# FFN up and gate projections by seven block products in place of eight

## The chip, the cores and the metric

The kernel runs on one core of a Trainium2 chip. The metric is the time of one execution on the device in microseconds (us). A core has TensorE (PE, matrix products into PSUM banks), VectorE (DVE), ScalarE (ACT), GpSimd (POOL) and SyncE (SP), whose queue issues nearly all transfers between the device's memory and the core's SBUF. Each engine runs its own queue in order and waits on semaphores.

## The reference

One layer of a hybrid decoder for a prompt of 2048 tokens and 8 single-token samples, model width 1024, FFN width 2816, in float32. The part that the change touches:

```python
h = rmsnorm(x, g_ffn) * (1.0 + scale_f) + shift_f
u = h @ w_up_conv
gv = h @ w_up_gate
uc, s_conv_ffn_new = causal_dwconv(u, s_conv_ffn, conv_ffn_w, conv_ffn_b)
f = (jax.nn.gelu(uc) * gv) @ w_down
x = x + gate_f * f
```

Ahead of it stand an input projection (`w_in`), a retention block over chunks of 128 tokens, an RG-LRU block and an output projection (`w_out`).

## The kernel before

Tokens are in three groups of 704, 640 and 704 + 8 columns (groups 0, 1 and 2 below), each cut into two token blocks of 352, 320 and 356 columns. A group runs through the whole layer before the next one starts; features are on the partitions, tokens on the free axis.

A float32 product is made of three passes. Each operand is split into a high part, rounded to the format in which TensorE runs fast, and the low rest. `mm3` (L284) adds high x high, high x low and low x high into one bank. For an output tile of 128 rows and a token block, `proj` (L508) does so for eight k of 128 features: 24 matmuls.

Weights come in units of 512 KB, two ahead of their use. In group 0 `fetch` (L245) loads the unit, ScalarE makes the high part (L277), GpSimd the low one (L278), and SyncE stores both (1 MB) in device memory (L281); groups 1 and 2 load that 1 MB (L250). SyncE's store waits for GpSimd, with later loads behind it.

The FFN works on 22 tiles, two of which make a pair `i`. `up_item` (L799) takes a product out of its bank on ScalarE, does the convolution on VectorE (L809) and GeLU on ScalarE; `gate_item` (L821) multiplies it with the gate product and splits the result (L366 on ScalarE, L367 on GpSimd). `down_item` (L736) multiplies a pair's two tiles with `w_down` for one of 8 output tiles m and one block, 6 matmuls, and adds the result to x (L745 on VectorE). Down of pair i - 1 stands between the items of pair i.

At the FFN's start `norm2` (L774) sums the squares, forms the norm factor, spreads it with a small product (`bc2`), and `hnorm` (L468) makes the two parts of h. Block 1's operands are made while TensorE works on block 0 of the first two tiles (four items). The order of each engine's queue comes from a list of items in program order (`group_items`, L883), priorities and a scheduler's own model. The next group's x is brought in and transposed by `xload` (L416), listed at pair 4, into buffers of its own.

## Time and profile before

| | us |
|---|---|
| median of 3 runs | 2534.19 (2534.02 to 2536.27) |
| the profiled execution, whole | 2540.24 |
| its span, first to last instruction | 2538.3 |

The profile has the busy time of each engine, its share of the span, and groups of instructions by line: out <- in by the program's names, partitions x elements, count, then busy us and mean ns of one, then the engine's idle time just before them and what ended it. PEclk is the granted clock of TensorE as a share of the full one. Durations of matmuls overlap, so the pace of a stretch is its length over its count.

### The profile page before, as it was taken

The numbers are of one execution on the slowest core, as the hardware profiler recorded it, in microseconds if no ns is written. First come the engines' busy times: TensorE is split into PE (matmuls) and PEld (weight loads), VectorE is DVE, ScalarE is ACT, GpSimd is POOL, SyncE is SP. The second block draws the span as 40 slices with busy tenths as digits, with TensorE's granted clock in tenths as the row PEclk, the third lists the DMA queues.
The fourth block names the chain that finished last, engine by engine and source line by source line (L and its number), as shares of the span: only waits on it lengthen the run. The fifth ranks groups of instructions, "written<-read, shape, count | busy, mean of one in ns | idle before, by whom it ended". The sixth has DMA issues, their size and how long they took to land. (4 is left out here: it accounts for less than half of the span.)

```text
span 2538.3 us, 38920 instructions
## 1 busy us (share of the span) xinstructions
PE 2467.1 (97%) x15875; PEld 2388.5 (94%) x15875; DVE 1283.0 (51%) x3009; ACT 728.2 (29%) x1422; POOL 667.3 (26%) x641
## 2 busy tenths in 40 slices
PE   6999999999999999999999999999999899999997
PEld 4888888999999999999999999999998899999997
DVE  4744578433433465558433333456676734334335
ACT  4422345233233242224311111322222421111112
POOL 2444445343343342223100000222222300000010
PEclk8999999999999999999999999999999999999999
DMA  9575655666566553342444444353332243333432
GB/s 328 160 262 195 211 177 199 219 209 206 183 224 209 173 200 120 133 152 101 171 150 149 150 149 150 133 191 118 126 118 101 93 158 117 150 133 117 150 138 92
DMA packets 143223, 413.39 MB, mean 163 GB/s; under 512 B 8281, under 2 KB 88293, under 8 KB 105405
## 3 DMA queue, kind: packets, MB, share of 16 engines
q1 hardware_dynamic: 141943, 410.15, 46.5%
q8 instruction: 125, 2.05, 0.3%
q10 hardware_dynamic: 974, 0.49, 0.1%
q14 instruction: 53, 0.43, 0.1%
q0 software_dynamic: 128, 0.26, 0.0%
HBM read 297.18 MB, written 113.82 MB: 162 GB/s over the span
## 5 line engine op out<-in xcount | busy, mean ns | idle before, releaser
L285 PE MATMUL proj<-hh,w 128*128 128x352 f32 (+2 forms) x3264 | 1049.7, 323 | 14.0 <-DVE hh L504 7.3
L286 PE MATMUL proj<-hl,w 128*128 128x352 f32 (+2 forms) x3264 | 1051.0, 322 | 4.6 <-DVE hl L486 2.6
L287 PE MATMUL proj<-hh,w 128*128 128x352 f32 (+2 forms) x3264 | 1046.3, 321 | 0.0
L285 PEld LDWEIGHTS proj<-hh,w 128*128 128x128 f32 x3264 | 616.5, 189 | 25.9 <-ACT hh L491 7.9
L286 PEld LDWEIGHTS proj<-hl,w 128*128 128x128 f32 x3264 | 615.7, 189 | 10.8 <-DVE hl L486 4.9
L287 PEld LDWEIGHTS proj<-hh,w 128*128 128x128 f32 x3264 | 616.6, 189 | 1.0 <-issue 0.4
L745 DVE SCALAR_TENSOR_TENSOR x<-down,mod,x 128x352 f32<-128x352 f32 (+3 forms) x720 | 409.1, 570 | 206.0 <-PE down L287 204.8
L285 PE MATMUL down<-ffh,w 128*128 128x352 f32 (+2 forms) x1056 | 342.8, 325 | 8.2 <-DVE x L745 8.0
L367 POOL TENSOR_TENSOR ffl<-cv,ffh 128x352 fp32r<-128x352 f32 (+2 forms) x132 | 123.7, 937 | 822.8 <-ACT ffh L366 822.8
L287 PE MATMUL down<-ffh,w 128*128 128x352 f32 (+2 forms) x1056 | 338.5, 321 | 0.0
L286 PE MATMUL down<-ffl,w 128*128 128x352 f32 (+2 forms) x1056 | 338.4, 320 | 0.0
L278 POOL TENSOR_TENSOR w<-wr,w 128x1024 fp32r<-128x1024 f32 x96 | 232.0, 2423 | 364.6 <-ACT w L277 333.6
L807 DVE COPY oc<-u 128x2 f32<-128x2 f32 x132 | 37.0, 280 | 347.0 <-ACT u L804 347.0
L825 DVE TENSOR_TENSOR cv<-cv,proj 128x352 f32<-128x352 f32 (+2 forms) x132 | 67.4, 510 | 283.4 <-PE proj L287 281.4
L285 PEld LDWEIGHTS down<-ffh,w 128*128 128x128 f32 x1056 | 199.9, 189 | 10.8 <-DVE x L745 10.1
L804 ACT ACTIVATE u<-proj 128x352 f32<-128x352 f32 (+2 forms) x132 | 60.4, 458 | 512.9 <-PE proj L287 512.9
L286 PEld LDWEIGHTS down<-ffl,w 128*128 128x128 f32 x1056 | 200.2, 190 | 0.0
L287 PEld LDWEIGHTS down<-ffh,w 128*128 128x128 f32 x1056 | 200.0, 189 | 0.0
L277 ACT ACTIVATE w<-wr 128x1024 fp32r<-128x1024 f32 x98 | 102.6, 1056 | 262.7 <-issue 108.3
L809 DVE SCALAR_TENSOR_TENSOR cv<-u,vec,cv 128x352 f32<-128x352 f32 (+3 forms) x264 | 155.9, 591 | 33.7 <-ACT cv L805 27.2
L366 ACT ACTIVATE ffh<-cv 128x352 fp32r<-128x352 f32 (+2 forms) x132 | 64.3, 487 | 223.3 <-DVE cv L825 223.3
L818 ACT ACTIVATE cv<-cv 128x352 f32<-128x352 f32 (+2 forms) x132 | 64.6, 490 | 154.6 <-DVE cv L809 122.2
(220 smaller groups left out, 2630.3 us busy)
## 6 DMA issues: line engine op xcount, KB each, us to landing
w<-w_in SPq DMA_DIRECT2D x48, 1024.0 KB
w<-w_up_conv SPq DMA_DIRECT2D x44, 1024.0 KB
w<-w_up_gate SPq DMA_DIRECT2D x44, 1024.0 KB
w<-w_down SPq DMA_DIRECT2D x44, 1024.0 KB
w_in<-w SPq DMA_DIRECT2D x24, 1024.0 KB
w_up_conv<-w SPq DMA_DIRECT2D x22, 1024.0 KB
w_up_gate<-w SPq DMA_DIRECT2D x22, 1024.0 KB
w_down<-w SPq DMA_DIRECT2D x22, 1024.0 KB
```

The lines of the kernel that those rows point to most:

```text
L277: S.activation(out=wh, in_=r_, func=AF.Copy)
L278: lo_on.tensor_tensor(out=wl, in0=r_, in1=wh.bitcast(F32), op=ALU.subtract)
L285: T.matmul(out, wh, xh, start=first, stop=False)
L286: T.matmul(out, wh, xl, start=False, stop=False)
L287: T.matmul(out, wl, xh, start=False, stop=last)
L366: S.activation(out=hi[:, 0:n], in_=src, func=AF.Copy)
L367: G.tensor_tensor(out=lo[:, 0:n], in0=src, in1=hi[:, 0:n].bitcast(F32), op=ALU.subtract)
L745: V.scalar_tensor_tensor(out=xs, in0=q[:, 0:np_], scalar=modv[:, jg, m, 0:1], in1=xs, op0=ALU.mult, op1=ALU.add)
L804: S.activation(out=u[:, 2:2 + n], in_=q, func=AF.Copy)
L809: V.scalar_tensor_tensor(out=cv[:, 0:np_], in0=u[:, j:j + np_], scalar=cfw[:, j, ft:ft + 1], in1=cv[:, 0:np_], op0=ALU.mult, op1=ALU.add)
L818: S.activation(out=cv[:, 0:n], in_=cv[:, 0:n], func=AF.Gelu_apprx_tanh)
L825: V.tensor_tensor(out=cv, in0=cv, in1=q, op=ALU.mult)
```

## The change

Weights and h of a pair are taken as 2 x 2 blocks: A11, A12 (first tile; k 0 to 3 and 4 to 7), A21, A22 (second tile); b11, b21 (token block 0, the two halves of k), b12, b22 (block 1). Seven products of sums give all four outputs (tile, block): S1 = A21 + A22, S2 = S1 - A11, S3 = A11 - A21, S4 = A12 - S2 on the weights' side, t1 = b12 - b11, t2 = b22 - t1, t3 = t2 - b11, t4 = b21 - t2 on the other. Each is four k, 12 matmuls. P1, P6, P7 and P4 add up in bank x, P5 and P3 in bank z, P2 in bank y; P1, P5 and P6's running sums are copied out by ScalarE and added on VectorE (`quad_item`).

The sums of weights are made on VectorE in group 0 and stored split, 512 KB per operand, seven per pair and kind; all weights go in such half-size blocks, in a ring of eight, and four are fetched ahead. `operands1` makes b11 and b21 while block 1 is still in the output projection; `operands2` makes the other five from block 1. Down of a pair is spread over the next pair's first ten products. The groups are cut to 688, 680 and 680 + 8 columns (blocks of 344, 340 and 344), which makes six pieces of at most 128 tokens in each. x, h, the heads and the operands share nine buffers; the next group's x comes in after the last product of pair 10, and only its row statistics (`xstats`) at pair 4.

```diff
-LOOK, RAWS, UNITS = 2, 3, 4
-HOW0, HOW1, HOW2 = "vmvmvmvm", "pmpmpmpm", "vvmpmpmp"
+LOOK, RAWS, RING = 4, 7, 8
+HOW0, HOW1, HOW2 = "vmvmvmvm", "pmpmpmpm", "vpvpvpvp"
...
-    (0, 704, 0, (0, 352, 704)),
-    (704, 640, 0, (0, 320, 640)),
-    (1344, 704, NB, (0, 356, 712)),
+    (0, 688, 0, (0, 344, 688)),
+    (688, 680, 0, (0, 340, 680)),
+    (1368, 680, NB, (0, 344, 688)),
...
+PRODUCTS = {"P1": ("A11", "b11", "x", True), "P5": ("S1", "t1", "z", True), "P6": ("S2", "t2", "x", False),
+            "P2": ("A12", "b21", "y", True), "P7": ("S3", "t3", "x", False), "P3": ("S4", "b22", "z", False),
+            "P4": ("A22", "t4", "x", False)}
...
-    wp = ctx.enter_context(tc.tile_pool(name="w", bufs=UNITS))
-    xp = ctx.enter_context(tc.tile_pool(name="x", bufs=4))
-    hp = ctx.enter_context(tc.tile_pool(name="h", bufs=1))
+    wp = ctx.enter_context(tc.tile_pool(name="w", bufs=RING))
+    xp = ctx.enter_context(tc.tile_pool(name="x", bufs=9))
...
+            S.activation(out=w[:, 0:512], in_=src, func=AF.Copy)
+            lo_on.tensor_tensor(out=w[:, 512:1024], in0=src, in1=w[:, 0:512].bitcast(F32), op=ALU.subtract)
+            nm = "_".join(str(v) for v in key)
+            split[key] = dp.tile([P, 1024], F32, tag=nm, name=nm)
+            nc.sync.dma_start(out=split[key], in_=w.bitcast(F32))
...
+        if nm == "S1":
+            total("S1", A("A21"), A("A22"), ALU.add)
+            total("S2", pr["S1"], A("A11"), ALU.subtract)
+        elif nm == "S2":
+            total("S4", A("A12"), pr["S2"], ALU.subtract)
+        elif nm == "S3":
+            total("S3", A("A11"), A("A21"), ALU.subtract)
+        units[key] = parts(key, block(), A(nm) if nm[0] == "A" else pr[nm])
...
+        def hilo(g, nm, k, src, eng):
+            S.activation(out=g.hi(nm, k), in_=src, func=AF.Copy)
+            eng.tensor_tensor(out=g.lo(nm, k), in0=src, in1=g.hi(nm, k).bitcast(F32), op=ALU.subtract)
...
+            for k in range(KC):
+                r_ = g.raw32(k)
+                g.h2(k, b[0], n, bc, r_, HOW2[k])
+                g.hilo("b11" if k < 4 else "b21", k % 4, r_, V if HOW2[k] == "p" else G)
+                yield
...
+            for k in range(4):
+                r = []
+                for u in range(2):
+                    r_ = ttile("h32")[:, 0:n]
+                    g.h2(4 * u + k, b[0], np_, bc, r_, "vp"[u])
+                    if tails:
+                        V.tensor_copy(r_[:, np_:n], tails[u][:, k, :])
+                    r.append(r_)
+                t1, b22 = r
+                b11, b21 = g.raw32(k), g.raw32(4 + k)
+                V.tensor_tensor(out=t1, in0=t1, in1=b11, op=ALU.subtract)
+                t2 = ttile("t2")[:, 0:n]
+                V.tensor_tensor(out=t2, in0=b22, in1=t1, op=ALU.subtract)
+                yield
+                g.hilo("t1", k, t1, V)
+                g.hilo("t2", k, t2, V)
+                t3 = ttile("t3")[:, 0:n]
+                V.tensor_tensor(out=t3, in0=t2, in1=b11, op=ALU.subtract)
+                t3s.append(t3)
+                yield
+                V.tensor_tensor(out=b21, in0=b21, in1=t2, op=ALU.subtract)
+                g.hilo("b22", k, b22, G)
+                g.hilo("t4", k, b21, G)
+                yield
+            g.op["t3"] = slot("op", F32R)
+            for k, t3 in enumerate(t3s):
+                g.hilo("t3", k, t3, G)
...
+                mm3(q, wh[:, k, :], wl[:, k, :], g.hi(nm, k), g.lo(nm, k), start and k == 0, k == 3, not start)
+            return q
...
+        def quad_item(g, st, kind, i, what, out):
+            left, right, bank, start = PRODUCTS[what]
+            q = g.product(st, (kind, i, left), right, bank, start)
+            if what == "P1":
+                st["p1"] = g.keep(q, "p1")
+            elif what == "P5":
+                st["p5"] = g.keep(q, "p5")
+            elif what == "P6":
+                st["u2"] = g.keep(q, "u2")
+            elif what == "P2":
+                out(2 * i, 0, q, st.pop("p1"))
+            elif what == "P7":
+                out(2 * i + 1, 1, q, st.pop("p5"))
+            elif what == "P3":
+                out(2 * i, 1, q, st.pop("u2"))
+            else:
+                out(2 * i + 1, 0, q, None)
...
+            if more is None:
+                S.activation(out=u[:, 2:2 + n], in_=q, func=AF.Copy)
+            else:
+                V.tensor_tensor(out=u[:, 2:2 + n], in0=q, in1=more[:, 0:n], op=ALU.add)
...
+            if more is not None:
+                V.tensor_tensor(out=more[:, 0:n], in0=q, in1=more[:, 0:n], op=ALU.add)
+                q = more[:, 0:n]
...
-        def up(ft):
-            for b in g.blocks:
-                add([("w_up_conv", P * ft)] if b == g.blocks[0] else [], 1, g.up_item, ft, b)
-            for b in g.blocks:
-                add([("w_up_gate", P * ft)] if b == g.blocks[0] else [], 1, g.gate_item, ft, b)
-        def dn(i, blocks):
-            ks = [("w_down", P * 2 * i), ("w_down", P * (2 * i + 1))]
-            for b in blocks:
-                for m in range(KC):
-                    add(ks if (b, m) == (g.blocks[0], 0) else [], 1,
-                        lambda b=b, m=m: g.down_item(ks, [g.fft[2 * i], g.fft[2 * i + 1]], 5, b, m))
+        quads = {}
+        def quad(kind, i, what, rate=1):
+            st = quads.setdefault((kind, i), {})
+            out_fn = g.up_out if kind == "w_up_conv" else g.gate_out
+            add([(kind, i, PRODUCTS[what][0])], rate, g.quad_item, st, kind, i, what, out_fn)
...
+        UP, GATE = "w_up_conv", "w_up_gate"
+        for what in ("P1", "P2"):
+            quad(UP, 0, what, 3)
+        for what in ("P1", "P2"):
+            quad(GATE, 0, what, 3)
+        add([], 0, lambda: drain(soon))
+        for kind in (UP, GATE):
+            for what in ("P5", "P6", "P7", "P3", "P4"):
+                quad(kind, 0, what)
...
+        both = [(b, m) for h in range(2) for b in g.blocks for m in range(4 * h, 4 * h + 4)]
+        seq = ("P1", "P5", "P6", "P2", "P7", "P3", "P4")
         for i in range(1, np_):
             if nxt is not None and i == 4:
-                add([], 0, lambda: bg.append(nxt.xload()))
-            up(2 * i)
-            if i < np_ - 1:
-                dn(i - 1, g.blocks)
-                up(2 * i + 1)
-            else:
-                dn(i - 1, g.blocks[:1])
-                up(2 * i + 1)
-                if nxt is not None:
-                    def start():
-                        drain(bg)
-                        nxt.halloc()
-                        soon.extend(nxt.norm1(b, HOW1) for b in nxt.blocks)
-                    add([], 0, start)
-                dn(i - 1, g.blocks[1:])
+                add([], 0, lambda: bg.append(nxt.xstats()))
+            d = dn(i - 1, both) if i < np_ - 1 else []
+            for n, (kind, what) in enumerate((kind, what) for kind in (UP, GATE) for what in seq):
+                quad(kind, i, what)
+                take = 0 if n < 1 else 1 if n < 2 else 2
+                out.extend(d[:take])
+                d = d[take:]
+        if nxt is not None:
+            def start():
+                drain(bg)
+                soon.append(nxt.xload())
+                soon.append(nxt.hstart())
+                soon.extend(nxt.norm1(b, HOW1) for b in nxt.blocks)
+            add([], 0, start)
+        out.extend(dn(np_ - 2, both, 2))
```

VectorE's queue in group 1, where block 1's operands are made. Before (h32 is the normed block, hl its low part, cv and u the convolution of pair 0's tiles, oc the convolution's carried columns):

```order
L482 SCALAR_TENSOR_TENSOR h32_11861<-x_5541,mod_114,bc_11859 128x320
L482 SCALAR_TENSOR_TENSOR h32_11865<-x_5541,mod_114,bc_11859 128x320
L482 SCALAR_TENSOR_TENSOR h32_11901<-x_5541,mod_114,bc_11859 128x320
L482 SCALAR_TENSOR_TENSOR h32_11911<-x_5542,mod_114,bc_11859 128x320
L803 COPY u_11943<-oc_112 128x2
L486 SCALAR_TENSOR_TENSOR hl_8538<-h32_11861,mod_114,hh_8537 128x320
L807 COPY oc_112<-u_11943 128x2
L809 SCALAR_TENSOR_TENSOR cv_11944<-u_11943,vec_104,cv_11944 128x320
L482 SCALAR_TENSOR_TENSOR h32_11957<-x_5542,mod_114,bc_11859 128x320
L486 SCALAR_TENSOR_TENSOR hl_8538<-h32_11865,mod_114,hh_8537 128x320
```

And with the change, the first of four k (keep holds block 0's h, op_13228 is t1 and op_13230 is t2, split):

```order
L889 SCALAR_TENSOR_TENSOR h32_13234<-x_9589,mod_111,bc_13232 128x340
L938 TENSOR_TENSOR h32_13234<-h32_13234,keep_13079 128x340
L940 TENSOR_TENSOR t2_13241<-h32_13237,h32_13234 128x340
L894 TENSOR_TENSOR op_13228<-h32_13234,op_13228 128x340
L946 TENSOR_TENSOR t3_13247<-t2_13241,keep_13079 128x340
L949 TENSOR_TENSOR keep_13079<-keep_13079,t2_13241 128x340
L1003 TENSOR_TENSOR u_13264<-qy_13251,p1_13207 128x340
L894 TENSOR_TENSOR op_13230<-t2_13241,op_13230 128x340
```

One operation per k and a low part have become a chain of seven, with the first output (L1003) between them.

TensorE's queue at the same place. Before, behind the spread of block 1's norm factor come whole products of block 0 (hh and hl hold both blocks; w2 is a unit):

```order
L794 MATMUL bc2_11840<-dg_11850,ones_92 128x128
L794 MATMUL bc2_11840<-dg_11853,ones_92 128x128
L794 MATMUL bc2_11840<-dg_11856,ones_92 128x64
L285 MATMUL proj_11969<-hh_8537,w2_11869 128x320
L286 MATMUL proj_11969<-hl_8538,w2_11869 128x320
L287 MATMUL proj_11969<-hh_8537,w2_11869 128x320
```

With the change one product of block 0 is left there (P2 of the gate, 12 matmuls into qy_13333), and behind it the first k of P5 (qz) and P6 (qx) of both kinds take turns, from its last matmul on:

```order
L348 MATMUL qy_13333<-op_13078,wb_12930 128x340
L346 MATMUL qz_13388<-op_13228,wb_13192 128x340
L347 MATMUL qz_13388<-op_13228,wb_13192 128x340
L348 MATMUL qz_13388<-op_13228,wb_13192 128x340
L346 MATMUL qx_13194<-op_13230,wb_13249 128x340
L346 MATMUL qz_13487<-op_13228,wb_13403 128x340
L347 MATMUL qz_13487<-op_13228,wb_13403 128x340
L348 MATMUL qz_13487<-op_13228,wb_13403 128x340
L347 MATMUL qx_13194<-op_13230,wb_13249 128x340
```

So TensorE reaches operands of block 1 after less work of block 0, and takes them one k at a time.

SyncE's queue in the steady FFN of group 0 (wr: a raw weight; a name in the place of the target: a split block stored). Before:

```order
L256 DMA wr_6045<-in_w_down 128x1024
L281 DMA w_up_conv1280_5908<-w2_5905 128x2048
L256 DMA wr_6120<-in_w_down 128x1024
L281 DMA w_up_gate1280_5983<-w2_5980 128x2048
L273 DMA wr_6187<-in_w_up_conv 128x8x128
L281 DMA w_down1024_6050<-w2_6047 128x2048
```

And with the change:

```order
L281 DMA w_up_gate_5_A22_7094<-wb_7091 128x1024
L262 DMA wr_7201<-in_w_down 128x512
L281 DMA w_up_conv_6_A11_7123<-wb_7118 128x1024
L281 DMA w_up_conv_6_S1_7155<-wb_7152 128x1024
L268 DMA wr_7224<-in_w_up_conv 128x4x128
L281 DMA w_down_1280_0_7180<-wb_7175 128x1024
L281 DMA w_down_1408_0_7205<-wb_7200 128x1024
L281 DMA w_up_conv_6_S2_7231<-wb_7228 128x1024
```

Loads and stores took turns; now there are more stores than loads, each of half the size, and several stores follow one another.

More of the change, by code (lines that the diff above doesn't have):

```diff
@@ L275, in fetch @@
[L275 to L287 removed]
+        elif kind == "w_ada":
+            r_ = [load_rows_of(kind, key[2] * P, a * D + 512 * h) for h in range(2)]
+            units[key] = [r_[h][:, c:c + 256] for h in range(2) for c in (0, 256)]
+        elif kind == "w_down":
+            units[key] = parts(key, block(), None if key in split else load_rows_of(kind, a, 512 * key[2]), lo_on)
+        elif kind in ("w_in", "w_out"):
+            both = []
+            for h in range(2):
+                r_ = None
+                if key + (h,) not in split:
+                    r_ = load_rows_of(kind, a, 512 * h) if kind == "w_out" else load_cols_of(kind, a, h)
+                both.append(parts(key + (h,), block(), r_, lo_on))
+            units[key] = [(both[k // 4][0][:, k % 4, :], both[k // 4][1][:, k % 4, :]) for k in range(KC)]
+        else:
+            fetch_operand(key)
@@ new lines, in fetch_operand, with A, total @@
+    def fetch_operand(key):
+        kind, i, nm = key
+        if key in split:
+            units[key] = parts(key, block())
+            return
+        pr = pairs.setdefault((kind, i), {})
+        def A(n):
+            if n not in pr:
+                pr[n] = load_cols_of(kind, P * (2 * i + int(n[1]) - 1), int(n[2]) - 1)
+            return pr[n]
+        def total(n, x, y, op):
+            pr[n] = rtile("ws")
+            V.tensor_tensor(out=pr[n], in0=x, in1=y, op=op)
+        if nm == "S1":
[6 more added lines that the diff above has]
+        units[key] = parts(key, block(), A(nm) if nm[0] == "A" else pr[nm])
+        if i == 0 and nm in ("A11", "A12"):
+            del pr[nm]
@@ L289, in hybrid_step, with mm3 @@
+    def mm3(out, wh, wl, xh, xl, first, last, more=False):
+        T.matmul(out, wh, xh, start=first, stop=False, skip_group_check=more)
+        T.matmul(out, wh, xl, start=False, stop=False, skip_group_check=more)
+        T.matmul(out, wl, xh, start=False, stop=last, skip_group_check=more)
     ada_ps = {}
@@ L795, in norm2 @@
             yield
[L796 to L807 removed]
+            yield from (g.operands1 if b == g.blocks[0] else g.operands2)(b, bc)
@@ new lines, in product, with keep @@
+        def product(g, st, key, nm, bank, start):
+            wh, wl = units.pop(key)
+            if start:
+                st[bank] = pst("q" + bank)
+            q = st[bank][:, 0:g.n]
+            for k in range(4):
+                mm3(q, wh[:, k, :], wl[:, k, :], g.hi(nm, k), g.lo(nm, k), start and k == 0, k == 3, not start)
+            return q
+        def keep(g, q, name):
+            t = ttile(name)
+            S.activation(out=t[:, 0:g.n], in_=q, func=AF.Copy)
+            return t
@@ L985, in group_items @@
             add([], 0, small_outputs)
-        for b in g.blocks:
-            dn(np_ - 1, [b])
+        last = dn(np_ - 1, [(b, m) for b in g.blocks for m in range(KC)])
+        for n, b in enumerate(g.blocks):
+            out.extend(last[KC * n:KC * n + KC])
             add([], 0, lambda b=b: soon.append(g.final(b)))
@@ L1018, in hybrid_step, with weight @@
     order = [key for it in items for key in it[0]]
+    def weight(key):
+        return 2 if key[0] in ("w_in", "w_out", "w_ada") else 1
     got, credit, seen = 0, 0.0, 0
@@ L1051, in hybrid_step @@
         seen += len(keys)
-        while got < len(order) and got < seen + LOOK:
+        while got < len(order) and sum(weight(k) for k in order[seen:got]) < LOOK:
             fetch(order[got])
```

224 lines of the change are left out of this document (140 added, 84 removed).

## Prediction

> **What bounds the kernel now.** I read the page first: the busy shares, and the rate of the DMA engines in 40 slices.
>
> ```profile
> span 2538.3 us, 38920 instructions
> ...
> PE 2467.1 (97%) x15875; PEld 2388.5 (94%) x15875; DVE 1283.0 (51%) x3009; ACT 728.2 (29%) x1422; POOL 667.3 (26%) x641
> ...
> GB/s 328 160 262 195 211 177 199 219 209 206 183 224 209 173 200 120 133 152 101 171 150 149 150 149 150 133 191 118 126 118 101 93 158 117 150 133 117 150 138 92
> ```
>
> Then the busy time of each engine in chosen stretches: the start of the program, the three FFN starts (380, 1183, 1985), the two changes of group (870, 1650) and the steady FFN of each group (500, 1250, 2100).
>
> ```profile
> core 0: us, PE busy (x) PEld busy (x) DVE busy (x) ACT busy (x) POOL busy (x), PEclk, DMA share, GB/s
> 0.00:50.00 50.00, 32.83 (x231) 20.08 (x232) 18.58 (x50) 22.09 (x50) 13.27 (x19) 0.90 1.01 334
> 380.00:425.00 45.00, 39.65 (x241) 37.62 (x241) 38.04 (x64) 27.94 (x61) 25.19 (x22) 0.92 0.53 175
> 500.00:850.00 350.00, 350.00 (x2176) 350.00 (x2176) 137.89 (x273) 103.03 (x164) 135.62 (x74) 1.00 0.63 204
> 870.00:900.00 30.00, 26.74 (x153) 25.85 (x152) 18.90 (x28) 13.37 (x28) 14.28 (x13) 0.92 0.26 106
> 1183.00:1220.00 37.00, 34.17 (x246) 32.66 (x245) 29.85 (x66) 25.58 (x62) 15.68 (x18) 1.00 0.36 128
> 1250.00:1600.00 350.00, 350.00 (x2387) 350.00 (x2387) 136.09 (x300) 61.92 (x131) 28.09 (x32) 1.00 0.41 151
> 1650.00:1680.00 30.00, 25.48 (x169) 25.10 (x168) 22.21 (x48) 12.16 (x29) 9.57 (x12) 0.94 0.41 146
> 1985.00:2035.00 50.00, 40.02 (x230) 38.14 (x230) 32.50 (x86) 23.08 (x50) 16.45 (x15) 0.90 0.29 107
> 2100.00:2450.00 350.00, 350.00 (x2153) 350.00 (x2152) 139.28 (x380) 58.83 (x117) 26.81 (x28) 1.00 0.36 135
> ```
>
> In the steady FFN TensorE is never idle and its granted clock is 1.00. Time there is a count of matmuls times a pace: 350/2176 = 160.8 ns at 352 columns, 146.6 ns at 320, 162.6 ns at 356. Thirty-two columns cost 14.2 ns, 0.444 ns each, so I put 344 columns at 157.3 ns and 340 at 155.5 ns. A matmul taken away is worth its pace, as long as nothing else becomes late.
>
> The FFN starts are the weak places. Idle time plus the share of clock withheld gives 5.4 + 3.6 = 9 us lost in group 0 and 3 us in group 1; in group 2, 230 matmuls at 162.6 ns fill 37 of 50 us, 12 us lost. The three lose 24 us now.
>
> **The products.** The matmuls of up, gate and input projection stand in one group of lines:
>
> ```profile
> L285 PE MATMUL proj<-hh,w 128*128 128x352 f32 (+2 forms) x3264 | 1049.7, 323 | 14.0 <-DVE hh L504 7.3
> ```
>
> Three such lines make 9792, of which up and gate have 22 x 2 tiles x 6 blocks x 24 = 6336. Afterwards they have 11 pairs x 2 x 7 products x 12 = 1848 per group, 5544 in all, 792 fewer. In time: 1056 x 2 x (0.1608 + 0.1466 + 0.1626) = 992.6 us before, 1848 x (0.1573 + 0.1555 + 0.1573) = 868.8 us after, **-124 us**. The new block widths sum to 1028 like the old ones, so other projections keep their time.
>
> **The new cut of the groups** gives group 1 a sixth piece: four more retention chunks (one per head) and 16 more transposes.
>
> ```profile
> 1004.23 0.27 PE L545 MATMUL kvT<-cst,head 128*128 128x128 f32 x1
> ...
> 1004.66 0.27 PE L545 MATMUL kvT<-cst,head 128*128 128x128 f32 x1
> ...
> 1007.76 0.38 PE L562 MATMUL o<-vt,sT 128*128 128x128 f32 x2
> ...
> 1008.42 0.27 PE L545 MATMUL kvT<-cst,head 128*128 128x128 f32 x1
> ```
>
> A chunk's first part takes 0.43 us of TensorE from start to start, its second 0.33 (two in 0.66), and a transpose 0.11 by the same rows: 4 x 0.9 + 16 x 0.11 = **+5 us**.
>
> **Getting sums out of the banks.** Each pair adds six vector additions out of PSUM and six scalar copies.
>
> ```profile
> L825 DVE TENSOR_TENSOR cv<-cv,proj 128x352 f32<-128x352 f32 (+2 forms) x132 | 67.4, 510 | 283.4 <-PE proj L287 281.4
> ...
> L804 ACT ACTIVATE u<-proj 128x352 f32<-128x352 f32 (+2 forms) x132 | 60.4, 458 | 512.9 <-PE proj L287 512.9
> ```
>
> VectorE had 137.89/350 of a pair's 46.3 us, 18 us; with 3 us more it has about half of 41.5 us. P6 adds onto bank x, which ScalarE must have copied after P1; P5 stands between, 12 x 157 ns = 1.9 us against 0.46 us. P4 waits for VectorE's read of x, with P3 between. I cost this at **nothing**; without that cover two waits of some 0.6 us come per kind and pair, 26 us in each group.
>
> **The FFN starts.** This is the largest price. Until the sums of block 1 exist, TensorE has P1 and P2 of both kinds: 48 x 0.1555 = 7.5 us. Before, it had four whole items of block 0, 96 matmuls. The norm before them is timed in group 1 from the last residual update to the copy of the norm factors:
>
> ```profile
> 1189.91 0.54 DVE L745 SCALAR_TENSOR_TENSOR x<-down,mod,x 128x320 f32<-128x320 f32 x1
> ...
> 1202.51 0.44 ACT L473 ACTIVATE bc<-bc 128x320 f32<-128x320 f32 x1 [0.32 <-PE bc L794]
> ```
>
> From the update's end to the end of the copy that is 12.5 us, with other work in the queues; less the 7.5 us of matmuls, 0 to 5 us stay open. I take 4, near the measured end. In TensorE's queue P3, P7 and the next pair's P1 stand behind the waiting P5 and P6 and cannot pass. Then the loop over four k runs: one scalar_tensor_tensor and six tensor_tensor on VectorE, three tensor_tensor on GpSimd, all from SBUF. The rows on such operations are minimum, median and longest duration in ns, and pieces of the timeline of group 0:
>
> ```profile
> L770 DVE TENSOR_TENSOR sq<-sq x36: 473/511/1259, 364.5 to 1996.5; 128x352 f32<-128x352 f32 x12, 128x320 f32<-128x320 f32 x12, 128x356 f32<-128x356 f32 x12
> L745 DVE SCALAR_TENSOR_TENSOR x<-down,mod,x x720: 507/579/591, 152.3 to 2522.3; 128x352 f32<-128x352 f32 x60, 128x320 f32<-128x320 f32 x60, 128x356 f32<-128x356 f32 x30, 128x348 f32<-128x348 f32 x30
> ...
> L367 POOL TENSOR_TENSOR ffl<-cv,ffh x132: 868/948/1233, 415.8 to 2497.0; 128x352 fp32r<-128x352 f32 x44, 128x320 fp32r<-128x320 f32 x44, 128x356 fp32r<-128x356 f32 x44
> ...
> 385.26 0.51 DVE L770 TENSOR_TENSOR sq<-sq 128x352 f32<-128x352 f32 x1
> 385.69 0.57 DVE L745 SCALAR_TENSOR_TENSOR x<-down,mod,x 128x352 f32<-128x352 f32 x1
> ...
> 390.25 2.22 DVE L482 SCALAR_TENSOR_TENSOR h<-x,mod,bc 128x352 f32<-128x352 f32 x1
> ...
> 389.42 2.68 POOL L278 TENSOR_TENSOR w<-wr,w 128x1024 fp32r<-128x1024 f32 x1
> ```
>
> L745, which reads PSUM, is never longer than 0.59 us in 720 times. L770 and L482, with both operands in SBUF, stretch to the end of a GpSimd operation that runs beside them (390.25 + 2.22 against 389.42 + 2.68). So the loop's VectorE work, 0.5 + 6 x 0.43 = 3.1 us from start to start, and GpSimd's, 3 x 0.93 = 2.8 us, exclude each other: 5.9 us per k, where TensorE has 12 matmuls, 1.9 us. Three gaps of 4 us, 4 us ahead, 2 us for t3, which GpSimd splits last: 18 us in group 1. In group 0 four weight splits of 1.3 us on GpSimd fall in between (23 us), in group 2 some 14 short operations on the sample columns (20 us). 61 against 24: **+37 us**. Were the two engines free of each other, a gap would be 1.2 us, a start 10 us, and the term +6; with the norm at its worst and GpSimd's queue later, I allow +55. I take the exclusive value, since each long row above fits it.
>
> The Trainium skill (SBUF — State Buffer, section Who interferes with whom) has the same rule: a VectorE instruction with two SBUF inputs and a GpSimd one that reads SBUF block each other fully. By it the term is +37, without it +6.
>
> **Weights in group 0.** Here blocks are formed, split and stored.
>
> ```profile
> w<-w_up_conv SPq DMA_DIRECT2D x44, 1024.0 KB
> ...
> w_up_conv<-w SPq DMA_DIRECT2D x22, 1024.0 KB
> ...
> wr<-in_w_up_conv SPq DMA_DIRECT2D x22, 512.0 KB
> ...
> more<-in_w_ada SPq DMA_DIRECT2D x14, 512.0 KB
> ...
> SPq L281 <- POOL w L278: 590.0, 89, 19.7
> ...
> ACT w L277 <- DMA wr<-in_w_in: 47.9, 13, 8.8
> ```
>
> Per pair, six units moved 6 x (0.52 + 1.05) = 9.4 MB, which at 204 GB/s is the 46.3 us of a pair. Now 18 half-size blocks are stored (9.4 MB) and 12 quarters of a MB read (3.1 MB): 12.6 MB in 264 x 0.1573 = 41.5 us, 303 GB/s. The present mix costs 0.63/0.204 = 3.09 us of the 16 engines per MB, so 39 of 41.5 us. GpSimd has 18 splits at 1.3 us (between 0.95 us for 352 columns and 2.4 us for 1024) and four of 0.95, 27 us. Nothing is over its limit, but a store at the head of SP's queue waits for GpSimd (590 us in 89 waits) and holds the loads behind it; behind a late load ScalarE's split waits (up to 8.8 us), and behind that the copy of P1 that P6 needs. I take 1.5 us per pair, **+16 us**. Bounds: 0, and 262 GB/s (the page's fastest slice after the first), 48 us per pair, +72.
>
> The Trainium skill (DMA: Bandwidth & Descriptors, section Measured) speaks against the change: batch to 1 MiB for 75% of peak. Its fit, 2.0 us plus bytes at 436 GB/s, gives an estimate of 164 GB/s for single transfers of 512 KB. The row of 0 to 50 us differs: 334 GB/s in transfers of 512 KB and less.
>
> Groups 1 and 2 load 9.4 MB per 41.5 us, 227 GB/s; at 0.36/0.135 = 2.67 us per MB that is 25 us, hidden.
>
> **Changes of group.** The next group's x can be brought in only when the operands' buffers are free: six pieces fall into the last 32 down items (30 us), with their transposes, copies and norm. (Its rows are also read earlier for their statistics, 2.8 MB a group, beside steady FFN work with transfers to spare.) Now the changes lose 3.3 us idle and 2.4 us of clock, and 4.5 and 1.8 us. I add 3 us each, **+6** (0 to 20).
>
> **Sum.** -124 + 5 + 37 + 16 + 6 = -60 us. The profiled execution took 2540.2 us (span 2538.3), so 2480; the median of the runs shown is 6 us lower, so **2474 us**.
>
> **Rivals.**
> - *The operands are hidden.* If VectorE and GpSimd alternate with little loss and group 0's queues hold: -124 + 5 + 6 + 3 + 2 = -108, 2426 us. Against it stand the long rows of L770 and L482.
> - *Group 0 partly short of transfers.* At 262 to 290 GB/s the term is 20 to 72 us: 2480 to 2530 us. For it: no slice after the first reached 303, though none had so much to move.
> - *Slower, by transfers.* Same place, a lower rate. Without the 16 us the sum is -76; slower begins when group 0 loses 81 us, 7.4 us per pair, 48.9 us for 12.6 MB: below 257 GB/s. At 240 GB/s a pair takes 52.5 us, +121, 2579 us. Against it: 334 GB/s at the start.
>
> **How the numbers follow.** Forecast (2440 to 2500) 0.5; hidden (2410 to 2440) 0.22; partly short (2500 to 2529) 0.14; slower 0.1; within 0.2%, about what a measurement of this kernel can tell from no change, 0.04. The range 2418 to 2530 leaves out the slower and unchanged cases and the end of the hidden one. Faster 0.86, same 0.04, slower 0.1.
>
> **What would show it.** Right: a steady FFN of groups 1 and 2 with TensorE without idle time, 157 ns per matmul; starts with waits of P5 and P6 (bank tiles qz, qx) on VectorE's subtractions, some 20 us each; group 0's steady FFN at a DMA share above 0.85. Wrong: idle TensorE in groups 1 and 2 behind the additions; starts under 10 us; group 0's pairs above 45 us.

## The result, and the profile after

| | us | ratio to the kernel before |
|---|---|---|
| before, on the same chip | 2535.23 (2534.02 to 2540.61) | |
| after | 2513.41 (2508.62 to 2514.42) | 0.9906 (95%: 0.9887 to 0.9925) |
| after, the profiled execution: whole, span | 2514.42, 2512.3 | |

The change gains 22 us by the medians (19 to 29 by the interval of the ratio) where 60 were forecast. The page of after, its first lines and the rate of the DMA engines in 40 slices:

```profile
span 2512.3 us, 40048 instructions
...
PE 2395.7 (95%) x15145; PEld 2293.4 (91%) x15145; DVE 1465.1 (58%) x3121; ACT 877.4 (35%) x1944; POOL 840.6 (33%) x849
...
PEclk8999997999999999999799999999999989999999
...
GB/s 342 170 267 192 202 194 165 310 292 291 301 281 302 322 196 140 130 117 95 138 233 233 223 241 218 247 170 196 135 124 129 90 157 211 242 218 236 217 245 129
```

The busy time by stretches: the 55 us behind the last matmul of the out-projection in each group (the FFN starts), then the steady FFN of groups 0, 1 and 2.

```profile
core 0: us, PE busy (x) PEld busy (x) DVE busy (x) ACT busy (x) POOL busy (x), PEclk, DMA share, GB/s
380.60:435.60 55.00, 31.39 (x120) 26.41 (x120) 45.23 (x75) 33.67 (x79) 38.01 (x35) 0.66 0.41 143
1199.70:1254.70 55.00, 42.58 (x197) 37.73 (x197) 34.52 (x61) 25.18 (x60) 18.97 (x20) 0.75 0.42 143
2008.50:2063.50 55.00, 42.06 (x194) 36.89 (x194) 34.54 (x85) 25.71 (x60) 20.32 (x19) 0.78 0.42 144
450.00:850.00 400.00, 392.13 (x2461) 386.32 (x2460) 273.11 (x394) 185.18 (x406) 277.14 (x209) 1.00 0.82 294
1250.00:1600.00 350.00, 350.00 (x2251) 350.00 (x2250) 152.86 (x292) 88.70 (x218) 34.33 (x35) 1.00 0.67 229
2100.00:2450.00 350.00, 350.00 (x2229) 350.00 (x2228) 162.11 (x401) 86.03 (x215) 34.69 (x35) 1.00 0.67 231
```

The steady FFN of groups 1 and 2 is as forecast: TensorE is never idle, at 350/2251 = 155.5 and 350/2229 = 157.0 ns per matmul. The FFN starts are not: 197 matmuls in 55 us of group 1 are 29.5 us of work at the usual pace, so 25.5 us are lost. The same stretches of the kernel before:

```profile
386.30:441.30 55.00, 51.64 (x319) 49.90 (x318) 43.82 (x65) 31.71 (x65) 32.97 (x24) 0.94 0.52 180
1186.70:1241.70 55.00, 52.69 (x375) 51.44 (x374) 33.80 (x78) 29.12 (x69) 17.75 (x20) 1.00 0.46 168
1988.10:2043.10 55.00, 45.70 (x267) 44.12 (x266) 31.38 (x83) 22.99 (x50) 16.93 (x16) 0.91 0.31 116
```

To see where the whole span went, take the distance from the start of each TensorE instruction to the next one's start. The usual distance of its shape (the 30th percentile) is work; what goes beyond it is lost, whether TensorE was idle or ran at a lower clock. One measure for all stages, in us:

| | forecast | before | after | change |
|---|---|---|---|---|
| work | -119 (-124 + 5) | 2354.4 | 2234.2 | -120.2 |
| lost in the three FFN starts (55 us each) | +37 | 25.7 | 88.8 | +63.1 |
| lost in the 45 us ahead of each (out-projection) | 0 | 21.3 | 28.4 | +7.1 |
| lost in group 0's steady FFN | +16 | 2.6 | 18.7 | +16.1 |
| lost in the steady FFN of groups 1 and 2 | 0 | 4.0 | 5.9 | +1.9 |
| lost in the changes of group (last 35 us) | +6 | 14.9 | 16.6 | +1.7 |
| lost elsewhere (first 100 us, attention, end) | 0 | 103.0 | 107.5 | +4.5 |
| sum | -60 | | | -25.8 (spans: -26.0) |

Of the 34 us between forecast and measurement the starts have 26 and the out-projection 7. The longest waits of TensorE in after (waiting instruction <- releaser: us in total, times, longest):

```profile
PE qz L346 <- ACT op L893: 18.3, 12, 3.6
PE down L346 <- DVE x L820: 16.6, 19, 3.0
...
PE qx L347 <- DVE op L894: 6.6, 8, 1.3
PE qx L346 <- ACT op L893: 6.2, 1, 6.2
```

`qz` and `qx` are banks of the seven products, `op` the operands: P5, P6 and P1 wait for the split that ScalarE begins. `down` waits for VectorE's updates of x.

### The profile page after: what moved, and what is told of

Same layout as the page of the kernel before. It is cut to its first block, busy times and chain, and to the rows that moved or that the text cites. A ratio compares the mean times of both kernels' runs of the same rounds, so it can differ in the third digit from the quotient of the medians.

```text
span 2512.3 us, 40048 instructions
## 1 busy us (share of the span) xinstructions
PE 2395.7 (95%) x15145; PEld 2293.4 (91%) x15145; DVE 1465.1 (58%) x3121; ACT 877.4 (35%) x1944; POOL 840.6 (33%) x849
## 5 line engine op out<-in xcount | busy, mean ns | idle before, releaser
L820 DVE SCALAR_TENSOR_TENSOR x<-down,mod,x 128x344 f32<-128x344 f32 (+2 forms) x720 | 401.0, 569 | 329.9 <-PE down L348 324.7
L346 PE MATMUL proj<-hh,wb 128*128 128x344 f32 (+1 forms) x1152 | 377.5, 328 | 10.1 <-ACT bc L546 7.2
L348 PE MATMUL proj<-hh,wb 128*128 128x344 f32 (+1 forms) x1152 | 371.4, 322 | 0.0
L347 PE MATMUL proj<-hl,wb 128*128 128x344 f32 (+1 forms) x1152 | 370.9, 322 | 0.2 <-DVE hl L559 0.2
L346 PE MATMUL down<-ffh,wb 128*128 128x344 f32 (+1 forms) x1056 | 339.9, 328 | 13.9 <-DVE x L820 13.1
L347 PE MATMUL qx<-op,wb 128*128 128x344 f32 (+1 forms) x1056 | 343.3, 325 | 9.7 <-DVE op L894 6.6
L346 PE MATMUL qx<-op,wb 128*128 128x344 f32 (+1 forms) x1056 | 341.3, 325 | 10.3 <-ACT op L893 6.2
L348 PE MATMUL qx<-op,wb 128*128 128x344 f32 (+1 forms) x1056 | 340.4, 323 | 0.0
L347 PE MATMUL down<-ffl,wb 128*128 128x344 f32 (+1 forms) x1056 | 338.3, 321 | 0.0
L348 PE MATMUL down<-ffh,wb 128*128 128x344 f32 (+1 forms) x1056 | 337.9, 321 | 0.0
L278 POOL TENSOR_TENSOR wb<-wr,wb 128x512 fp32r<-128x512 f32 x170 | 231.8, 1374 | 159.1 <-ACT wb L277 145.0
L346 PEld LDWEIGHTS proj<-hh,wb 128*128 128x128 f32 x1152 | 217.5, 189 | 19.9 <-ACT bc L546 7.3
L346 PEld LDWEIGHTS down<-ffh,wb 128*128 128x128 f32 x1056 | 198.6, 189 | 23.6 <-DVE x L820 22.4
L348 PEld LDWEIGHTS proj<-hh,wb 128*128 128x128 f32 x1152 | 217.6, 189 | 1.7 <-issue 0.9
L347 PEld LDWEIGHTS qx<-op,wb 128*128 128x128 f32 x1056 | 202.7, 192 | 13.8 <-DVE op L894 9.9
L346 PEld LDWEIGHTS qx<-op,wb 128*128 128x128 f32 x1056 | 202.4, 192 | 12.3 <-ACT op L893 6.8
L348 PEld LDWEIGHTS qx<-op,wb 128*128 128x128 f32 x1056 | 202.5, 192 | 0.1
L348 PEld LDWEIGHTS down<-ffh,wb 128*128 128x128 f32 x1056 | 200.1, 190 | 0.0
```

The lines of the kernel that those rows point to most:

```text
L278: lo_on.tensor_tensor(out=w[:, 512:1024], in0=src, in1=w[:, 0:512].bitcast(F32), op=ALU.subtract)
L346: T.matmul(out, wh, xh, start=first, stop=False, skip_group_check=more)
L347: T.matmul(out, wh, xl, start=False, stop=False, skip_group_check=more)
L348: T.matmul(out, wl, xh, start=False, stop=last, skip_group_check=more)
L820: V.scalar_tensor_tensor(out=xs, in0=q[:, 0:np_], scalar=modv[:, jg, m, 0:1], in1=xs, op0=ALU.mult, op1=ALU.add)
```

## The experiments

Each ran beside the kernel before on the same chip, in three rounds; by its ratio (0.9906) the changed kernel stands at 2515 to 2517 us there. The expectations speak of losses in stretches cut a little otherwise (some leave out the gap right behind the out-projection); below, all are by the measure of the table, each from one profiled execution.

### The new cut alone

In the kernel before, the lines of `GROUPS` alone are those of the change; buffers stay 712 wide.

```diff
-    (0, 704, 0, (0, 352, 704)),
-    (704, 640, 0, (0, 320, 640)),
-    (1344, 704, NB, (0, 356, 712)),
+    (0, 688, 0, (0, 344, 688)),
+    (688, 680, 0, (0, 340, 680)),
+    (1368, 680, NB, (0, 344, 688)),
```

> The kernel before with nothing but the new cut of the groups (688, 680, 680 + 8 columns). Theory A (the FFN starts took what the forecast misses): the cut costs the +5 us of the forecast, 2540 us, and the three FFN starts lose what they lose in the kernel before, about 44 us. Rival (the cut itself carries a good part of the 38 us that the forecast misses): 2555 us or more, with the loss in the input projection and retention of groups 1 and 2 or in the out-projection.

2549.13 us, ratio 1.0039 (1.0025 to 1.0054): 6 to 14 us, a little above the forecast's 5 and below the rival's 15. Work grows by 4.3 us, losses by 3.5. Starts and out-projections together lose 46.7 us, and 47.0 in the kernel before. So the cut does not carry what is missing in the starts.

### The sums left out, and more cover

What is the price of the chain that makes t1 to t4?

```diff
-                V.tensor_tensor(out=t1, in0=t1, in1=b11, op=ALU.subtract)
...
-                g.hilo("t2", k, t2, V)
...
+            g.op["t2"], g.op["t3"], g.op["t4"] = g.op["t1"], g.op["t1"], g.op["b22"]
```

> The changed kernel with the sums t1 to t4 of the second token block left out: only b12 and b22 are formed and split, and the products of the sums take these in their place, so the output is not the layer's. All matmuls stay. Theory A (a chain of VectorE and GpSimd operations that exclude each other sets the starts): a turn of the loop falls from 6.2 us to 2.9 us (two VectorE operations of 0.5 us and two GpSimd operations of 0.95 us), the last splits of 3.7 us go, and each start loses 15 to 17 us less: about 2465 us. Rival B (once TensorE's clock is halved by the gaps in P1 and P2, it stays slow whatever the operands do): less than 15 us in all, 2500 us or more.

And of the matmuls that no longer stand ahead of it? (Lines that only keep pair 1's blocks, give P2 a bank and take these products out of pair 1's list are left out.)

```diff
...
-        for what in ("P1", "P2"):
-            quad(UP, 0, what, 3)
-        for what in ("P1", "P2"):
-            quad(GATE, 0, what, 3)
+        for i in range(2):
+            for kind in (UP, GATE):
+                for what in ("P1", "P2"):
+                    quad(kind, i, what, 3)
...
```

> The changed kernel with P1 and P2 of pair 1, both kinds, moved ahead of the first P5, so that TensorE has 96 matmuls and not 48 that need nothing of the second token block. Theory D (the lost cover: the 7.5 us of matmuls that the change took from ahead of the operands are lost whole, in each start): 7.5 us less per start, about -22 us against the changed kernel, 2491 us where the kernel before takes 2535. Rival E (what the four more products leave behind, additions and convolutions on VectorE, sits in the queue of the operand chain and makes it as much longer): less than 8 us gained, 2505 us or more.

Then both edits at once:

> The kernel without the sums t1 to t4 (products take other operands in their place, so the output is not the layer's) and with P1 and P2 of pair 1 ahead of the first P5. Theory (the sums' chain and the lost cover are together the whole price of the FFN starts): the three starts lose 24 to 30 us together, as in the kernel before, where the run without the sums alone lost 47: 17 to 23 us less than that run, 2455 us. Rival (something else of the change stays in the starts): 37 us or more are lost, 2465 us or more.

| lost in the starts of groups 0, 1, 2 | | | | sum | ratio |
|---|---|---|---|---|---|
| before | 8.2 | 4.3 | 13.3 | 25.7 | 1 |
| after | 37.5 | 25.5 | 25.8 | 88.8 | 0.9906 |
| more cover | 32.7 | 19.2 | 21.8 | 73.8 | 0.9867 (0.9850 to 0.9884) |
| without sums | 27.4 | 12.6 | 14.2 | 54.2 | 0.9743 (0.9723 to 0.9763) |
| without sums, more cover | 18.8 | 4.1 | 9.3 | 32.2 | 0.9670 (0.9652 to 0.9687) |

The starts (columns as above) without the sums:

```profile
383.90:438.90 55.00, 37.10 (x184) 35.17 (x183) 37.88 (x60) 35.41 (x84) 41.48 (x36) 0.78 0.59 206
1191.60:1246.60 55.00, 50.83 (x281) 49.13 (x281) 27.30 (x53) 22.68 (x56) 14.24 (x14) 0.85 0.58 201
1985.60:2040.60 55.00, 46.16 (x269) 45.01 (x269) 27.67 (x76) 23.25 (x57) 13.48 (x14) 0.90 0.55 192
```

And without the sums, with more cover:

```profile
384.40:439.40 55.00, 45.51 (x239) 42.40 (x239) 45.90 (x64) 34.87 (x84) 43.35 (x35) 0.79 0.71 239
1178.70:1233.70 55.00, 52.58 (x338) 51.54 (x338) 31.66 (x60) 26.52 (x67) 15.01 (x15) 1.00 0.68 234
1962.80:2017.80 55.00, 49.11 (x300) 46.49 (x300) 30.52 (x81) 24.62 (x60) 14.71 (x15) 0.99 0.63 216
```

In group 1, 197 matmuls become 281 and then 338, and the clock comes back by itself. Taken out first, the sums cost 34.6 us; without them, the cover that the change took away is worth 22.0 us (8.6, 8.5 and 4.9), nearly three times the 7.5 us of 48 matmuls. What is left, 32.2 us, lies between the theory's 30 and the rival's 37, and is about what the kernel before loses too, but for group 0 (18.8 against 8.2). In the other order the prices differ: with the sums in place, the same cover recovers only 15.0 us in the starts, the time falls by about 10, and the sums are then worth 41.6.

Where in a start the time is lost follows from the first matmul of P5, which is the first that needs block 1. Ahead of it group 1 loses 7.8 us in after, 9.5 without the sums, 3.4 with more cover and 1.8 with both edits. In the 48 matmuls of the loop from there on it loses 15.5, 2.0, 15.6 and 1.3. So the cover works ahead of the loop and the sums' chain in it. Of the 48 matmuls of the cover only 36 come to stand ahead of P5 when the sums are there (102 matmuls in place of 66). That VectorE's queue holds up the rest, as rival E has it, is not shown.

What TensorE waits for ahead of P5 in group 1 of after is the last update of x, the copy of block 1's norm factors, and the first sum:

```profile
1200.23 0.57 DVE L820 SCALAR_TENSOR_TENSOR x<-down,mod,x 128x340 f32<-128x340 f32 x1 [0.81 <-PE down L348]
...
1213.27 0.46 ACT L917 ACTIVATE bc<-bc 128x340 f32<-128x340 f32 x1 [7.78 <-PE bc L869]
...
1216.82 0.42 PE L346 MATMUL qz<-op,wb 128*128 128x340 f32 x1 [1.67 <-ACT op L893]
```

From the update's end to the copy's end it is 12.9 us, against 12.5 in the kernel before: the norm is as long as ever. Another 3.1 us pass until t1 is formed and split and P5 starts. In group 0 the norm took longer already before the change, 17.1 us by the same two rows:

```profile
389.76 0.57 DVE L745 SCALAR_TENSOR_TENSOR x<-down,mod,x 128x352 f32<-128x352 f32 x1
...
406.94 0.47 ACT L473 ACTIVATE bc<-bc 128x352 f32<-128x352 f32 x1 [0.28 <-PE bc L794]
```

### Which engine makes the operands

```diff
-                    g.h2(4 * u + k, b[0], np_, bc, r_, "vp"[u])
+                    g.h2(4 * u + k, b[0], np_, bc, r_, "vv"[u])
...
-                g.hilo("b22", k, b22, G)
-                g.hilo("t4", k, b21, G)
+                g.hilo("b22", k, b22, V)
+                g.hilo("t4", k, b21, V)
...
-                g.hilo("t3", k, t3, G)
+                g.hilo("t3", k, t3, V)
```

> The changed kernel with all of the second block's operand work on VectorE, none of it on GpSimd; every value is the same. Theory A (the two engines exclude each other, 6.2 us a turn): VectorE alone needs eleven operations of about 0.45 us, 5.0 us a turn, and the last four splits 1.7 us in place of 3.7: 7 to 8 us less per start, 2490 us. Rival C (the two engines run beside each other, and the turn is long for another reason): three more operations on VectorE's queue make a turn 1.2 us longer, 2525 us.

2505.17 us, ratio 0.9868 (0.9852 to 0.9884): some 10 us gained, not 24; VectorE does more and the starts lose less (78.6 us in place of 88.8), so rival C falls. VectorE in the second turn of the changed kernel's loop in group 1, from the timeline (start, us, engine, line):

```profile
1222.08 0.51 DVE L938 TENSOR_TENSOR h<-h,keep 128x340 f32<-128x340 f32 x1
1222.69 0.51 DVE L940 TENSOR_TENSOR t<-h,h 128x340 f32<-128x340 f32 x1
1223.31 1.11 DVE L946 TENSOR_TENSOR t<-t,keep 128x340 f32<-128x340 f32 x1
1224.35 1.22 DVE L949 TENSOR_TENSOR keep<-keep,t 128x340 f32<-128x340 f32 x1
```

And GpSimd at the same time:

```profile
1223.14 0.91 POOL L894 TENSOR_TENSOR op<-h,op 128x340 fp32r<-128x340 f32 x1 [1.95 <-ACT op L893]
1224.13 1.06 POOL L886 TENSOR_TENSOR h<-x,bc 128x340 f32<-128x340 f32 x1
```

L946 and L949 end 0.4 us behind the GpSimd operations that began ahead of them: 1.11 and 1.22 us for what takes 0.51 alone. The first subtraction of the four turns in group 1 (minimum, median and longest in ns, first and last start), in after:

```profile
L938 DVE TENSOR_TENSOR h<-h,keep x4: 505/715/1135, 1215.7 to 1233.8; 128x340 f32<-128x340 f32 x4
```

The same with VectorE alone:

```profile
L938 DVE TENSOR_TENSOR h<-h,keep x4: 501/503/513, 1215.6 to 1231.8; 128x340 f32<-128x340 f32 x4
```

Alone it is not stretched in any of the four turns. A turn takes (1233.8 - 1215.7) / 3 = 6.0 us in after and 5.4 here. I expected 5.0: besides the eleven operations, additions and convolutions of pair 0 stand in the same queue, as in these rows of the first turn (VectorE alone):

```profile
1217.54 0.50 DVE L949 TENSOR_TENSOR keep<-keep,t 128x340 f32<-128x340 f32 x1
1217.96 0.50 DVE L1003 TENSOR_TENSOR u<-qy,p 128x340 f32<-128x340 f32 x1
...
1220.62 0.57 DVE L1023 SCALAR_TENSOR_TENSOR cv<-u,vec,cv 128x340 f32<-128x340 f32 x1
```

Then the first block's operands too:

```diff
-HOW0, HOW1, HOW2 = "vmvmvmvm", "pmpmpmpm", "vpvpvpvp"
+HOW0, HOW1, HOW2 = "vmvmvmvm", "pmpmpmpm", "vvvvvvvv"
...
-                g.hilo("b11" if k < 4 else "b21", k % 4, r_, V if HOW2[k] == "p" else G)
+                g.hilo("b11" if k < 4 else "b21", k % 4, r_, V)
```

> The changed kernel with the operand work of both token blocks on VectorE (the run before had the second block's alone); every value is the same. Theory F (the first block's operands, made by the two engines in turn while the out-projection still runs, hold up its updates of x, and so 10 us of the 13 lost there): the out-projection's last 45 us lose 6 to 10 us less in all three groups, 2497 us where the run before took 2505. Rival G (it is the longer wait for the norm, or the cut, and sixteen operations more or less on VectorE change nothing or hold the updates longer): 2505 us or more.

2499.28 us, ratio 0.9844 (0.9829 to 0.9859). Against the run before, the out-projections lose 4.2 us less (26.4 to 22.2), the starts 1.4 more; the intervals overlap. By the losses, theory F has the direction, at half its size; the time alone does not tell it from rival G. Its mechanism shows in the changed kernel, on VectorE and on TensorE:

```profile
1191.08 4.76 DVE L889 SCALAR_TENSOR_TENSOR keep<-x,mod,bc 128x340 f32<-128x340 f32 x4 [0.54 <-ACT bc L901]
1195.76 0.56 DVE L820 SCALAR_TENSOR_TENSOR x<-down,mod,x 128x340 f32<-128x340 f32 x1
...
1196.37 0.42 PE L346 MATMUL down<-mrh,wb 128*128 128x340 f32 x1 [2.98 <-DVE x L820]
```

Four operations for b11, 1.2 us each beside GpSimd, stand ahead of an update of x, and TensorE waits 3 us for its bank.

### The withheld clock

The granted clock falls to 0.66 to 0.78 in the starts. Is that a cause?

```diff
+                fill = psm("fill")
+                for j in range(12):
+                    T.matmul(fill[:, 0:n], g.hi("b11", j % 4)[:, 0:P], g.hi(("t1", "t2", "t4")[j // 4], k),
+                             start=True, stop=True)
```

> The changed kernel with twelve matmuls per turn of the operand loop added, 48 in each FFN start, into a bank that nothing reads. They take operands that exist already and fill TensorE's gaps; 7.5 us of work per start at full clock. Theory A (the operands set the length of the start): the stretches at half clock get shorter, and the time stays within 8 us of the changed kernel, 2505 to 2521 us. Rival B (the withheld clock sets it): each start gains up to 17 us of clock less the fill's 7.5, 2485 us.

The starts of this kernel:

```profile
381.60:436.60 55.00, 35.24 (x172) 31.51 (x171) 45.35 (x75) 33.66 (x79) 38.20 (x35) 0.78 0.41 143
1201.60:1256.60 55.00, 45.62 (x248) 42.68 (x248) 34.77 (x62) 25.75 (x61) 19.94 (x20) 0.89 0.43 143
2008.20:2063.20 55.00, 45.16 (x254) 42.12 (x254) 35.88 (x87) 25.80 (x60) 19.53 (x19) 0.93 0.43 145
```

The clock rises in all three and 48 matmuls more fit in, but the time is 2512.76 us, ratio 0.9898 (0.9883 to 0.9913): unchanged. The length of the loop shows why. From the first matmul of P5 to the end of the 48 it takes 26.1, 23.0 and 22.4 us in after, and 25.7, 22.6 and 21.7 here, with 44 of the added matmuls in between and a granted clock of 0.87 to 0.92 in place of 0.58 to 0.62. So in the loop the operands set the pace, the clock falls because TensorE waits, and it costs next to nothing of its own. Ahead of the loop the clock is low too, and no run fills the gaps there.

The Trainium skill (TensorE: Matmul & The Clock Gate, section HAM oscillation — how this bites in real kernels) counts half of the throttled time as lost. The mean granted clock went from 0.971 to 0.983, by which that rule gives an estimate of 0.012 x 2512 = 30 us gained. The added matmuls are 22.5 us of work, which would leave 8 us net; the measured 2 us, with some 6 us of interval either way, does not exclude that. Against the rule, for the loop, speaks its length.

### Group 0's steady FFN

Its 16 us came out in size, but the profile shows another mechanism than the forecast's. TensorE's waits in after from 450 to 850 us:

```profile
PE down L346 <- DVE x L820: 6.0, 11, 1.2
PE qx L346 <- DVE u L1003: 1.4, 1, 1.4
```

VectorE's longest waits there:

```profile
DVE ws L330 <- DMA wr<-in_w_up_gate: 58.8, 10, 10.0
DVE x L820 <- PE down L348: 23.4, 28, 2.1
```

The first list is whole: TensorE waits for VectorE alone. `ws` at L330 are the weights' sums: at the head of VectorE's queue they wait for loads, and updates of x stand behind them. Four edits take the explanation apart. No addition:

```diff
-            pr[n] = rtile("ws")
-            V.tensor_tensor(out=pr[n], in0=x, in1=y, op=op)
+            pr[n] = x
```

> The changed kernel with the additions that form the weights' sums left out: a block is split and stored in the place of each sum, so the output is not the layer's. Every transfer, split and matmul stays; VectorE has eight operations fewer per pair in group 0, 6 to 10 us of its 41. Theory H (group 0's steady part loses its 16 us behind VectorE): it loses 6 us or less, 2503 us. Rival I (it loses them to the transfers, as the forecast had it): no change there, 2510 us or more.

The addition on a constant:

```diff
-            V.tensor_tensor(out=pr[n], in0=x, in1=y, op=op)
+            res = ident[:, 0:P].unsqueeze(1).to_broadcast([P, 4, P])
+            V.tensor_tensor(out=pr[n].rearrange("p (k c) -> p k c", c=P), in0=res, in1=res, op=op)
```

> The changed kernel with the weights' sums formed by the same additions on VectorE, but from a constant that has been in SBUF since the start, so that an addition waits for no load; the output is not the layer's. All loads, splits, stores and matmuls stay. Theory H1 (in group 0 the addition waits for its load at the head of VectorE's queue, 64 us by the profile, and the updates of x behind it hold TensorE): the steady part of group 0 loses less than 8 us where the changed kernel lost 19: about 2505 us. Theory H2 (it is the additions' own time, about 1.1 us each, stretched beside GpSimd's splits): it still loses 14 us or more, and the time is within 5 us of the changed kernel's 2517 (with the kernel before at 2541).

The addition on GpSimd:

```diff
-            V.tensor_tensor(out=pr[n], in0=x, in1=y, op=op)
+            G.tensor_tensor(out=pr[n], in0=x, in1=y, op=op)
```

> The changed kernel with the weights' sums formed on GpSimd and not on VectorE; every value is the same. Theory H1: a sum that waits for its load now holds only splits and no update of x; GpSimd has 43 of 50 us to do; the steady part of group 0 loses less than 8 us, 2505 us. Rival J (GpSimd, with 8 more operations of 1.2 us per pair, and the operations of VectorE that it shuts out, is what TensorE then waits for): 2517 us or more.

And no addition (the first edit), with this:

```diff
-LOOK, RAWS, RING = 4, 7, 8
+LOOK, RAWS, RING = 4, 4, 8
```

> The changed kernel without the additions that form the weights' sums (blocks stand in their place, so the output is not the layer's) and with 4 buffers for loaded blocks in place of 7: a pair uses 12 of them and not 20, so the loads run no further ahead than in the changed kernel (a third of a pair). Theory H2 (VectorE's time for the additions, with what they wait for, is what group 0's steady part lacks): it loses less than 7 us, as without the additions alone (3 us). Rival K (the additions' buffers are the price: they hold up the loads): it loses 13 us or more, as the changed kernel did (19 us).

| | lost in group 0's steady FFN | ratio |
|---|---|---|
| after | 18.7 | 0.9906 (0.9887 to 0.9925) |
| no additions | 3.3 | 0.9819 (0.9803 to 0.9836) |
| additions on a constant | 14.6 | 0.9885 (0.9870 to 0.9900) |
| additions on GpSimd | 14.3 | 0.9920 (0.9899 to 0.9941) |
| no additions, 4 buffers | 15.4 | 0.9879 (0.9857 to 0.9901) |

One thing limits what this table can tell: in eight kernels whose weights' sums are made as in after (after itself and the runs on sums, cover, operands and clock, alone or together), this stretch loses between 13.0 and 22.6 us. So 14 to 15 is not told from 18.7, and 3.3 is. The profile of the additions on GpSimd is of an execution 6 us under that kernel's median.

Without the additions the loss is gone, with the same transfers; theory I, that transfers alone cost it, falls. But neither half of the explanation is enough alone. With no load to wait for, the additions still cost 14.6 us (H1 falls): they wait for GpSimd to free their buffers instead, and take 1.33 us each, as their group on VectorE shows:

```profile
L331 DVE TENSOR_TENSOR ws<-cst 128x512 f32<-128x512 f32 x76 | 100.3, 1333 | 32.5 <-POOL wb L278 28.9 <-DMA wr<-in_w_up_gate 3.4
```

And without additions, but with fewer buffers, another wait comes up, for the weights' own splits, which is close to the path that the forecast described:

```profile
PE qx L347 <- POOL wb L278: 3.6, 4, 1.1
PE qx L345 <- ACT wb L277: 1.7, 2, 1.0
```

So two limits lie close together in group 0, VectorE's queue and the buffers of loaded blocks; the additions load both. In the changed kernel it is VectorE's that TensorE meets. Which of the two would give more if the additions had to stay is open. On GpSimd, which is then busy for 371 of 400 us, they gain nothing: 2517.13 us is what rival J forecast, but TensorE's longest waits there are still for VectorE's updates of x, so J's reason is not shown.

### Edits that leave nothing out, together

The edits of more cover and of both blocks on VectorE:

> The changed kernel with both edits: P1 and P2 of pair 1 ahead of the first P5, and the operand work of both blocks on VectorE. If theories A, D and F hold and the gains add: -22 - 10 - 8 us, 2475 us where the kernel before takes 2535. If VectorE becomes what the starts wait for, the gains don't add: 2485 us or more.

These and the additions on GpSimd:

> Three edits together: P1 and P2 of pair 1 ahead of the first P5, the operand work of both blocks on VectorE, the weights' sums on GpSimd. If the gains add (23 us of the first two, 12 of the third): 2483 us with the kernel before at 2541. If GpSimd becomes group 0's bound: 2494 us or more.

More cover with all operand work on VectorE takes 2494.30 us, ratio 0.9816 (0.9800 to 0.9832), the lowest of the kernels that leave nothing out: 1.8% under the kernel before and 0.9% under the changed one. Its starts lose 65.6 us. The gains don't add, 23 us in place of the 40 expected. With the weights' sums on GpSimd too it is 2499.52 us, 0.9839 (0.9822 to 0.9856): the intervals overlap. Group 0's steady FFN then loses 26.0 us. GpSimd is less busy there (354 of 400 us) than with its additions alone (371), and TensorE's longest waits are for VectorE, so why it loses more stays open.

## Why the forecast was wrong, point by point

- **Products (-124) and new cut (+5): right.** Work fell by 120.2 us, of which the cut alone is +4.3; the paces came within 0.3 ns. The cut also brings 3.5 us of losses, which were not in the sum. (The rows shown for a chunk give 0.43 + 0.33 = 0.76 us and not the 0.9 of the sum; +5 stays.)
- **Sums out of banks (0): right.** The steady FFN of groups 1 and 2 shows no wait of TensorE.
- **FFN starts (+37): the step that failed.** Measured +63: the three starts lose 88.8 us, where the forecast had 61; the losses of the kernel before were read rightly (24 against 25.7). In the loop the three groups lose 18.6, 15.5 and 14.9 us, 49.0 against 43 forecast, and behind it 6.1 against 6. Ahead of it they lose 18.6, 7.8 and 7.3, 33.7 where "I take 4" gave 12. So 22 of the 28 us that are missing come from that step. It took the norm's 12.5 us less the 7.5 us of P1 and P2, for every group. The norm is as long as it was (12.9 in group 1), but what stands behind it was left out: from the copy of the norm factors to the first P5 it takes 4.6, 3.1 and 3.3 us. In groups 1 and 2 that is nearly the whole excess (3.8 and 3.3). The 96 matmuls that stood there before hid this chain; half of them went, and the runs with more cover show that the loss ahead of P5 follows their number. With both the sums undone and the cover restored, 32.2 us stay, about the 25.7 of the kernel before. In group 0 the norm was longer from the start (17.1 us before the change, 17.8 after), and the first P1 waits 6.2 us for b11 (the wait `qx <- op` above). The weights' additions are part of it: in the two runs without them group 0's start loses 33.0 and 30.7 us, in those that make them on a constant or on GpSimd 37.8 and 37.9, in after 37.5. What makes the rest of group 0's excess is open.
- **Out-projection (0): missed.** +7.1 us, 3 of them with the cut alone (24.3 against 21.3). Making block 0's operands on VectorE too recovers 4 (26.4 to 22.2), of which groups 1 and 2 keep theirs in the run with more cover (13.6 against 17.1); group 0 varies by as much from kernel to kernel. The prediction followed the new waits ahead of P5, not the updates of x that stand behind `operands1`.
- **VectorE and GpSimd exclude each other: right,** in the forecast's own place: the rows of L938, L946 and L949, and a turn of 6.0 us where 5.9 was forecast. The Trainium skill's rule (SBUF — State Buffer, section Who interferes with whom) holds here: 1.11 and 1.22 us beside GpSimd for what takes 0.51 alone. Avoiding it gains only some 10 us, since VectorE then has the work.
- **Weights in group 0 (+16): right size, wrong reason.** The DMA share is 0.82 (forecast 0.94) at 294 GB/s (303); the loads are late for VectorE's additions, not for ScalarE's splits, and TensorE waits for the updates of x behind them. That the size came out is luck in so far as this price was not in the sum. The estimate of 164 GB/s goes by the Trainium skill's fit for single transfers (DMA: Bandwidth & Descriptors, section Anatomy of one DMA — SWDGE (gpsimd) path). It is no bound here, where many transfers are under way: 294 GB/s.
- **Changes of group (+6): +1.7.**
- **Rivals.** Hidden operands, transfers that run short and a slower kernel: none came. The time lies where the second rival put it (2480 to 2530), for another reason: that is chance.

## What to carry to other kernels

When a change takes matmuls away, ask what they hid: those ahead of a serial chain are worth less than their pace. Here 15 to 22 of the 22.5 us that the change took from ahead of the three loops were lost again. Price a stage's start as the length of its chain, up to the first operand, less the work that remains to cover it, and read that length in each group. A low clock in such a stretch can be a sign of waiting and not a cause; here, filling the loop's gaps raised the clock and left the loop as long as it was.
